# The planner that orders all instructions of a hybrid attention layer gets new durations and a rule on VectorE and GpSimd

## The chip, the cores and the metric

One core of a Trainium2 chip runs the whole layer in one launch. The metric is the device time of one execution in microseconds, lowest is best; the number given for a kernel is the median of its runs. The profile is of one more execution, and it has a time of its own.

## The reference

The layer has 512 tokens of 1024 channels in float32. One RMS-normed input goes through one wide projection; two attention mixers read it, A with 8 heads and B with 8 heads in 2 groups; their outputs are gated, widened to 1024 channels, merged with two sigmoid gates, and projected once more onto the residual.

```python
h = rms_norm(x, norm_w[l])
proj = h @ w_in[l]
(q_a, k_a, v_a, z_a, q_b, kc, vc, ksl, vsl, kwn, vwn, gate_b, z_b, gate_m) = jnp.split(proj, split_points, axis=-1)
o_a = moba_mixer(rms_norm(heads(q_a), q_norm_a[l]), rms_norm(heads(k_a), k_norm_a[l]), heads(v_a), bias_a)
k_cmp = rms_norm(compress(heads(kc), cmp_pos_k[l], cmp_w1_k[l], cmp_w2_k[l]), k_norm_cmp[l])
v_cmp = compress(heads(vc), cmp_pos_v[l], cmp_w1_v[l], cmp_w2_v[l])
o_b = nsa_mixer(...)          # compressed + selected + window branch, each a softmax(q k + bias) v
y_a = o_a * jax.nn.silu(z_a)
y_b = o_b * jax.nn.silu(z_b)
g_m = jax.nn.sigmoid(gate_m)
merged = g_m[..., :D_MODEL] * (y_a @ w_branch_a[l]) + g_m[..., D_MODEL:] * (y_b @ w_branch_b[l])
x = x + merged @ w_out[l]
```

With 512 tokens the block choices of both mixers take in every past block, so A is 8 causal softmax attentions and B is, for each of its 8 heads, two causal softmax attentions (selected and window keys) and a small one over the compressed keys.

## The kernel before

**Arithmetic.** All large products are made as three products of a high and a low part: a weight tile `wr` (128x512) is rounded to `wh`, and `wl = wr - wh` is the rest; the activations are `hh` and `hl`. `mm3` (lines 298 to 312, all its matmuls have line 309) issues hh·wh, hh·wl and hl·wh into one PSUM tile.

**Streams of TensorE work.** Four Python generators issue the matmuls. `gemms` (F) makes the projections in a fixed list: token-major pieces (`pgf`, `pgt`: queries, keys, values), channel-major pieces (`pgc`: gates z and gm), the two widening products (`pbr`, of `yh`/`yl`) and the output (`po`). `attention` (A) walks over 24 units, one softmax attention each: transposed queries and keys (`pq`), scores `sps` for four blocks of query rows from the widest (512 keys) to the narrowest, transposes `pt` of the probabilities `P`, and products with the values into `O`. While unit n makes its scores, unit n-1 makes its transposes and products. `cmp` (C) is the compression of keys and values (`hps`: 16 tiles of `in_w` weights, one after the other, one raw buffer each), and `x_rms` (X) is the token norm.

**The work between matmuls.** Each PSUM tile is followed by a `Chain` of steps on the other engines. A softmax block: `sb` (scores plus bias tile `T`, VectorE, line 848, with the row maximum), exponential `P` (ScalarE, 863, with the row sum), reciprocal (VectorE, 866), scaling of `P` (GpSimd, 867), transposes on TensorE (876), `ph` (ScalarE, 888), `pl` (VectorE, 890), products `O` (910, 1054). A query or key piece: `nraw`, squares, `nss` (554, 353), the power -1/2 `nr` on GpSimd (354), two products `nxn` (556, 551), then high and low part of `qk` (532, 533). After the last product of a head: `ot` (ScalarE, 935), `ys` (939), gate product (949), `yh` (950), `yl` (951); `pbr` of mixer B needs this of all B heads. A weight tile: `wh` (280 or 282) and `wl` (284).

**Who sets the order.** Nothing is reordered by the compiler: `manual_schedule` fixes the order on every engine, and each engine runs its own list strictly in that order. The list is made while the kernel is built, by a small planner in the kernel itself. It keeps a clock `now`, the time at which each engine gets free (`free`), and gives each step a cost in ns; a step that may run on several engines goes to the one that would end first (`Chain.step`); after each step the chain goes on `OUT[engine] + LAT` ns later. The main loop gives the next piece of TensorE work to the stream that is ready and has had least time for its share (`SHARE_A`, `SHARE_F`, `SHARE_C`). The loop before is, in its core:

```python
ok = [r for r, w in ws if w is not None and w <= now[0]]
...
r = min(ok, key=lambda q: q.vt)
```

`W.split(...)`, called by `ahead`, decides how many weight tiles ahead of their use are split. All DMAs are issued by SyncE in the order in which the planner meets them. Four raw weight buffers (`NRAW`), eight split ones, two PSUM tiles for the projections, two for scores, three for transposes and one for `O` bound how far anything can run ahead.

Of the kernel before, what the change touches and what calls it, by code (L numbers as in the profile page):

```python
# [12 lines left out]
F32 = mybir.dt.float32  # L13
# [5 lines left out]
S = 512  # L19
# [22 lines left out]
LAT = 30  # L42
SHARE_A = 1.0
SHARE_F = 1.2
SHARE_C = 0.6
LAG = 20000
XR = 6000.0
XQ = 1200
# [38 lines left out]
def hybrid_kernel(ctx: ExitStack, tc: tile.TileContext, x, xT, norm_w, wtok, wchan, gains, w1,  # L87
# [24 lines left out]
    OUT = {"A": 140, "D": 160, "P": 80}  # L112
# [8 lines left out]
    ENG = {"A": nc.scalar, "D": nc.vector, "P": nc.gpsimd}  # L121
# [7 lines left out]
    def cd(n):  # L129
        return 65 + 1.045 * n  # L130

    def cg(n):
        return 65 + 2.27 * n

    def either(n):
        return {"D": cd(n), "P": cg(n)}

    class Chain:
# [29 lines left out]
        def step(c):  # L168
# [182 lines left out]
    def rsqrt_mean(c, dst, ss, n, w, parts=P):  # L351
        v = (lambda z: z() if callable(z) else z)
        c.do({"D": 70}, lambda e: e.tensor_scalar(v(ss), v(ss), 1.0 / n, EPS, op0=ALU.mult, op1=ALU.add))  # L353
        c.do({"P": 300 + 165 * w}, lambda e: e.tensor_tensor(v(dst), v(ss), mhalf[:parts, :w], op=ALU.pow))  # L354
# [18 lines left out]
    def x_split(k):  # L373
# [4 lines left out]
        c.do({"D": 602}, lambda e: e.scalar_tensor_tensor(hl[:, k, :], xts[k], w, hh[:, k, :].bitcast(F32),  # L378
# [30 lines left out]
    def x_rms():  # L409
# [6 lines left out]
        c = Chain(now[0] + 200)  # L416
        c.do({"D": 70}, lambda e: e.tensor_scalar(rx, ps[:, :NT], 1.0 / D, EPS, op0=ALU.mult, op1=ALU.add), ps)
        c.do({"P": 958}, lambda e: e.tensor_tensor(rx, rx, mhalf[:, :NT], op=ALU.pow))
# [19 lines left out]
    def x_rows():  # L438
# [6 lines left out]
        yield 432  # L445
        Chain(now[0] + 200).do({"A": 478}, lambda e: e.copy(R, ps), ps).mark("R")
# [49 lines left out]
    def gemm_first(name, emit, tags="ggss"):  # L496
# [4 lines left out]
        for k in range(KT):  # L501
            for a, b in ((0, 0), (1, 0), (0, 1)):
# [8 lines left out]
                yield n * 0.4217 * NT + 10  # L511
# [54 lines left out]
    def proj_norm(name, g0, tags="gggg"):  # L566
        toks[name] = [None] * NT

        def emit(t, ps):
            toks[name][t] = att(name)  # L570
            ch = Chain(now[0] + 200)
# [33 lines left out]
    def bias_rows():  # L605
# [28 lines left out]
    def compress_w(kv):  # L634
# [3 lines left out]
        def emit(ps):  # L638
            ch = Chain(now[0] + 200)
# [25 lines left out]
    def compress_h(kv):  # L665
# [4 lines left out]
        for q in range(8):  # L670
            ws = W1.take(1, 256)
            for i in range(2):
# [680 lines left out]
```

## Time and profile before

| | |
|---|---|
| median of 3 runs | 488.29 us (487.93 to 490.03) |
| the profiled execution's own time | 488.61 us |
| its span, first to last instruction | 486.8 us |
| busy share of the span | TensorE 98%, weight loads 88%, VectorE 70%, ScalarE 52%, GpSimd 41% |
| instructions | 8681, of them 3060 matmuls, 831 on VectorE, 625 on ScalarE, 248 on GpSimd |
| granted TensorE clock | 0.999 |

In the profile PE is TensorE's matmuls, PEld its weight loads, DVE is VectorE, ACT is ScalarE, POOL is GpSimd and SP is SyncE. Matmuls overlap in the record, so a busy PE is no proof that it loses nothing; what it loses is read from the waits, or from the distance between starts. "a <- b: 2.9, 5, 1.4" in the view of waits is 2.9 us in five waits of a for b, the longest 1.4 us. A row of the timeline has the start, the duration, the engine, line, operation and tiles, and in brackets the idle time ahead of it with what ended it.

### The profile page before, as it was taken

The page shows a single profiled execution, that of the slowest core. Times are in us where ns is not written, and L with a number is a line of the kernel's source. Part 1 is how long each engine was busy: PE and PEld are TensorE (multiplying, and loading weights), DVE is VectorE, ACT ScalarE, POOL GpSimd, SP SyncE. Part 2 cuts the span into 40 slices and gives each one's busy share as a digit, 9 for nine tenths or more (in the row PEclk, how much of TensorE's full clock was granted, in tenths as well). Part 3 has the DMA queues.
Part 4 walks back from the last instruction along what each step waited for, and adds up shares of the span by engine and source line. Part 5 has one row for each costly group of instructions (what it writes and reads, how often), then busy time and mean ns, then how long its engine had stood idle before and what let it go on. Part 6 is the DMA issues. An engine that isn't in the chain of part 4 may idle for free.

```text
span 486.8 us, 8681 instructions
## 1 busy us (share of the span) xinstructions
PE 474.8 (98%) x3060; PEld 426.5 (88%) x3060; DVE 338.5 (70%) x831; ACT 254.7 (52%) x625; POOL 198.5 (41%) x248
## 2 busy tenths in 40 slices
PE   7999898999999999999999999999999999999997
PEld 7999788999999989988888888888888888889997
DVE  5986898689988769897889777875555535444331
ACT  6565675477785346686675477765222332322210
POOL 4455587257786425856542355554211100110000
PEclk9999999999999999999999999999999999999999
DMA  8548153443343404022212222112223234554421
GB/s 273 160 120 171 42 144 110 131 111 115 110 130 109 131 22 132 22 74 60 65 45 82 92 56 58 42 43 66 65 88 105 91 108 141 148 166 142 140 89 43
DMA packets 28124, 49.16 MB, mean 101 GB/s; under 512 B 3312, under 2 KB 5744, under 8 KB 28080
## 3 DMA queue, kind: packets, MB, share of 16 engines
q1 hardware_dynamic: 28080, 48.60, 35.0%
q8 instruction: 24, 0.39, 0.3%
q14 instruction: 20, 0.16, 0.1%
HBM read 45.84 MB, written 2.75 MB: 100 GB/s over the span
## 4 chain that ended last, share of the span: by engine, by line
PE 73%; DVE 12%; POOL 5%; DMA 4%; issue 3%; ACT 2%; SPq 0%; DVEq 0%; ACTq 0%; POOLq 0%
PE pgc L309 26%; PE po L309 9%; PE pbr L309 9%; PE pgt L309 9%; PE O L910 5%; PE pt L876 5%; PE sps L829 3%; DVE wl L284 2%; PE sps L830 2%; POOL nr L354 2%; DMA rtab<-rt 2%; POOL P L867 1%; PE pq L761 1%; DVE nxn L556 1%; DVE sq L395 1%
## 5 line engine op out<-in xcount | busy, mean ns | idle before, releaser
L309 PE MATMUL pgc<-hh,wh 128*128 128x512 f32 x208 | 84.5, 406 | 0.0
L309 PE MATMUL pgt<-wh,hh 128*128 128x256 f32 (+1 forms) x288 | 82.3, 286 | 0.0
L309 PE MATMUL pgc<-hl,wh 128*128 128x512 f32 x208 | 81.9, 394 | 0.0
L309 PE MATMUL pgc<-hh,wl 128*128 128x512 f32 x208 | 81.8, 393 | 0.0
L284 DVE TENSOR_TENSOR wl<-wr,wh 128x512 fp32r<-128x512 f32 (+1 forms) x101 | 78.9, 784 | 3.6 <-ACT wh L280 3.1
L309 PE MATMUL pgt<-wl,hh 128*128 128x256 f32 (+1 forms) x288 | 81.3, 282 | 0.0
L309 PE MATMUL pgt<-wh,hl 128*128 128x256 f32 (+1 forms) x288 | 81.0, 281 | 0.0
L280 ACT CAST wh<-wr 128x512 fp32r<-128x512 f32 (+1 forms) x91 | 54.1, 616 | 22.9 <-DMA wr<-in_wout 18.1
L284 POOL TENSOR_TENSOR wl<-wr,wh 128x512 fp32r<-128x512 f32 x23 | 31.3, 1361 | 78.9 <-ACT wh L280 78.1
L867 POOL TENSOR_SCALAR P<-P,sst,gate 128x512 f32<-128x512 f32 (+3 forms) x56 | 40.6, 731 | 53.3 <-DVE sst L866 37.2
L848 DVE CUSTOM_DVE_ANT_0 sb<-sps,T 128x512 f32<-128x512 f32 (+3 forms) x96 | 46.3, 485 | 23.0 <-PE sps L830 19.5
L863 ACT ACTIVATE P<-sb,sst 128x512 f32<-128x512 f32 (+3 forms) x88 | 51.0, 580 | 10.8 <-DVE sst L848 7.5
L309 PEld LDWEIGHTS pgt<-wh,hh 128*128 128x128 f32 x288 | 54.2, 188 | 0.5
L309 PEld LDWEIGHTS pgt<-wh,hl 128*128 128x128 f32 x288 | 54.3, 188 | 0.4
L309 PEld LDWEIGHTS pgt<-wl,hh 128*128 128x128 f32 x288 | 54.2, 188 | 0.0
L888 ACT CAST ph<-pt 128x512 fp32r<-128x512 f32 (+2 forms) x72 | 33.6, 479 | 33.5 <-PE pt L876 32.8
L309 PEld LDWEIGHTS pgc<-hl,wh 128*128 128x128 f32 x208 | 39.1, 188 | 9.1
L309 PEld LDWEIGHTS pgc<-hh,wh 128*128 128x128 f32 x208 | 39.1, 188 | 7.2
L309 PEld LDWEIGHTS pgc<-hh,wl 128*128 128x128 f32 x208 | 39.2, 189 | 7.0
L876 PE MATMUL pt<-cst,P 128*128 128x128 f32 x232 | 40.9, 273 | 1.2 <-POOL P L867 1.1
L890 DVE TENSOR_TENSOR pl<-pt,ph 128x512 fp32r<-128x512 f32 (+2 forms) x72 | 38.4, 547 | 4.0 <-ACT ph L888 4.0
L354 POOL TENSOR_TENSOR nr<-nss,mhalf 128x4 f32<-128x4 f32 x28 | 31.0, 1109 | 21.0 <-DVE nss L353 19.3
(214 smaller groups left out, 1108.4 us busy)
## 6 DMA issues: line engine op xcount, KB each, us to landing
wr<-in_wchan SPq DMA_DIRECT2D x52, 256.0 KB, 2.7
wr<-in_wtok SPq DMA_DIRECT2D x36, 256.0 KB, 3.0
T<-rtab SPq DMA_DIRECT2D x16, 256.0 KB, 3.6
wr<-in_w SPq DMA_DIRECT2D x16, 256.0 KB, 2.7
wr<-in_wbr SPq DMA_DIRECT2D x16, 256.0 KB, 2.7
wr<-in_wout SPq DMA_DIRECT2D x16, 256.0 KB, 2.8
x<-in_xT SPq DMA_DIRECT2D x8, 256.0 KB, 4.9
xr<-in_x SPq DMA_DIRECT2D x8, 256.0 KB, 3.6
```

The costliest lines, as they stand in the source:

```text
L280: e.copy(hi, raw)
L284: c.do(either(n), lambda e, hi=hi, lo=lo, raw=raw: e.tensor_sub(lo, raw, hi.bitcast(F32))).mark((w, 1, i))
L309: nc.tensor.matmul(dst, sts[i][a], mvs[i][b], start=(start and i == a == b == 0), stop=(stop and i == n - 1 and b == 1))
L354: c.do({"P": 300 + 165 * w}, lambda e: e.tensor_tensor(v(dst), v(ss), mhalf[:parts, :w], op=ALU.pow))
L829: nc.tensor.matmul(sps[:, :n], qs[:, b * P:(b + 1) * P], ks[:, :n], start=True, stop=False)
L848: e.tensor_tensor_reduce(z["sb"][:, :L], sps[:, :L], T[:, S - L:], scale=-1.0, scalar=3e38, op0=ALU.add, op1=ALU.min, accum_out=st[:, 0, b ...
L863: e.activation(pv(), z["sb"][:, :L], AF.Exp, bias=st[:, 0, b:b + 1], scale=-1.0, accum_out=st[:, 1, b:b + 1])
L867: c.do({"P": 244 + 0.834 * L}, lambda e: e.tensor_scalar(pv(), pv(), st[:, 2, b:b + 1], g, op0=ALU.mult, op1=ALU.mult))
L876: nc.tensor.transpose(pt[:, (b - kb) * P:(b - kb + 1) * P], u.p0 if u.p0 is not None and b == 0 else u.pb[:, POFF[b] + kb * P:POFF[b] + (k ...
L888: e.copy(z["w"][0], pt[:, :w])
L890: ch.do({"D": cd(w)}, lambda e: e.tensor_sub(z["w"][1], pt[:, :w], z["w"][0].bitcast(F32)), pt)
L910: nc.tensor.matmul(O[0][:, S - n:], v.bitcast(F32) if kb == 3 else v, w, start=(u.first and kb == 0 and i == 0), stop=(u.last and kb == 3 ...
```

## The change

No operation is added or removed on TensorE, and no tile, buffer or precision changes. The planner's numbers and two of its rules change, and with them the order of nearly all instructions and the engine of some:

- Costs: GpSimd sums and products go from 65 + 2.27 n to 180 + 2.08 n ns, GpSimd powers from 300 + 165 w to 430 + 150 w, small GpSimd steps from 60 or 82 to 140 or 160, a matmul of n columns from 0.4217 n + 2.5 to 4.5 + 0.4427 n, four transposes from 224 to 340, the delay after TensorE from 200 to 230 ns. After a step a chain waits `OUT + LAT`: 170, 190 and 110 ns for ScalarE, VectorE and GpSimd before, 165, 145 and 90 now.
- Exclusion: steps marked "d" on VectorE and "P" on GpSimd (those that read SBUF operands) exclude each other in the planner's clock; powers and small steps on GpSimd are marked "p" and exclude nothing.
- Shares: F from 1.2 to 1.1 and C from 0.6 to 1.0. A stream counts as ready only when it has been so for 300 ns (`MARGIN`), else the one that has waited longest goes. In the widening products `ahead` counts to 2 instead of 4, so all four next weight tiles are split after the second product instead of two.

```diff
-LAT = 30
+LAT = 60
 SHARE_A = 1.0
-SHARE_F = 1.2
-SHARE_C = 0.6
+SHARE_F = 1.1
+SHARE_C = 1.0
+MARGIN = 300
...
-    OUT = {"A": 140, "D": 160, "P": 80}
+    OUT = {"A": 105, "D": 85, "P": 30}
...
+    lock = {"d": 0.0, "P": 0.0}
...
     def cg(n):
-        return 65 + 2.27 * n
+        return 180 + 2.08 * n
...
     def either(n):
-        return {"D": cd(n), "P": cg(n)}
+        return {"d": cd(n), "P": cg(n)}
+
+    def ends(k, t, n):
+        t = max(t, free[k.upper()])
+        if k in lock:
+            o = lock["d" if k == "P" else "P"]
+            return max(t + n, o + n - 55 if o > t else 0.0)
+        return t + n
...
-                k = min(cost, key=lambda k: max(free[k], c.t) + cost[k])
-                free[k] = max(free[k], c.t) + cost[k]
-                c.t = free[k] + OUT[k] + LAT
+                end, k = min((ends(k, c.t, n), k) for k, n in cost.items())
+                if k in lock:
+                    lock[k] = end
+                free[k.upper()] = end
+                c.t = end + OUT[k.upper()] + LAT
...
-        c.do({"P": 300 + 165 * w}, lambda e: e.tensor_tensor(v(dst), v(ss), mhalf[:parts, :w], op=ALU.pow))
+        c.do({"p": 430 + 150 * w}, lambda e: e.tensor_tensor(v(dst), v(ss), mhalf[:parts, :w], op=ALU.pow))
...
-                ahead((w + 1) / 4)
+                ahead((w + 1) / 2)
...
-        ok = [r for r, w in ws if w is not None and w <= now[0]]
+        ok = ([r for r, w in ws if w is not None and w + MARGIN <= now[0]] or
+              [r for r, w in sorted(((r, w) for r, w in ws if w is not None and w <= now[0]), key=lambda z: z[1])[:1]])
```

Counted over the whole program, TensorE has the same matmuls; VectorE has 31 steps more (17 of them `wl`, 10 `nxn`), GpSimd 37 fewer (17 `wl`, 10 `nxn`, 4 `XW`, 5 copies for `kf`, and others, against 4 more casts), ScalarE 6 more. Line numbers grow by 16 at the places below.

**VectorE, start of the attention.** `sps139` are the first scores, `T` their bias tile (read back from DRAM), `wl138` a weight tile, `nss135` and `nss147`, `nxn134` and `nxn146` the norms of the third and fourth token block of the second query and key piece `qk1`, which the transposes `pq157` need. Before:

```order
L848 ISA sb141_761,sst140_757<-sps139_751,T122_688 128x512
L848 ISA sst140_757 128x1
L284 TENSOR_TENSOR wl138_746<-wr105_611,wh137_745 128x512
L554 TENSOR_REDUCE nss135_738<-nxn134_737 128x4
L866 RECIPROCAL sst140_757<-sst140_757 128x1
L353 TENSOR_SCALAR nss135_738<-nss135_738 128x4
L533 TENSOR_TENSOR qk1109_646<-nxn112_653,qk1109_646 128x4x64
L554 TENSOR_REDUCE nss147_789<-nxn146_788 128x4
L353 TENSOR_SCALAR nss147_789<-nss147_789 128x4
```

Now:

```order
L300 TENSOR_TENSOR wl138_747<-wr105_610,wh137_746 128x512
L570 TENSOR_REDUCE nss135_738<-nxn134_737 128x4
L864 ISA sb141_772,sst140_767<-sps139_761,T123_698 128x512
L864 ISA sst140_767 128x1
L369 TENSOR_SCALAR nss135_738<-nss135_738 128x4
L570 TENSOR_REDUCE nss147_790<-nxn146_789 128x4
L369 TENSOR_SCALAR nss147_790<-nss147_790 128x4
L882 RECIPROCAL sst140_767<-sst140_767 128x1
```

The weight tile, one of the two sums and `qk1109` now stand ahead of the step that waits for `T`; on ScalarE the squares that the second sum reads, and on GpSimd both powers `nr136` and `nr148`, now stand ahead of the first exponential and the first scaling.

**VectorE, the last unit of the attention.** `sb1210` (before) and `sb1218` (now) are its last scores, `pl` the low parts of transposed probabilities, `pbr` a widening product, the two reciprocals those of its blocks of 384 and 256 keys. Before:

```order
L848 ISA sb1210_4908,sst1183_4824<-sps1205_4897,T1135_4659 128x256
L848 ISA sst1183_4824 128x1
L890 TENSOR_TENSOR pl1202_4887<-pt1199_4876,ph1201_4886 128x512
L890 TENSOR_TENSOR pl1207_4901<-pt1203_4890,ph1206_4900 128x384
L866 RECIPROCAL sst1183_4824<-sst1183_4824 128x1
L890 TENSOR_TENSOR pl1212_4915<-pt1208_4903,ph1211_4914 128x256
L866 RECIPROCAL sst1183_4824<-sst1183_4824 128x1
```

Now:

```order
L864 ISA sb1218_4954,sst1193_4873<-sps1210_4938,T1145_4710 128x256
L864 ISA sst1193_4873 128x1
L1222 SCALAR_TENSOR_TENSOR gm953_4017<-gm953_4017,pbr1188_4853 128x512
L906 TENSOR_TENSOR pl1212_4943<-pt1208_4932,ph1211_4942 128x384
L300 TENSOR_TENSOR wl1217_4951<-wr1164_4761,wh1216_4950 128x512
L882 RECIPROCAL sst1193_4873<-sst1193_4873 128x1
L906 TENSOR_TENSOR pl1220_4958<-pt1213_4945,ph1219_4957 128x256
L882 RECIPROCAL sst1193_4873<-sst1193_4873 128x1
```

A gate product and a weight tile now stand between the last scores and the reciprocals.

**TensorE, the end of the attention.** `pt` are the transposes of the last unit's probabilities, `O` its products, `pgc` a gate's projection, `pbr` the widening product. Before, after the last scores, two transposes, six `pgc`, eight steps of the unit before and three `pgc`, the last unit's transposes come, and then

```order
L876 MATMUL pt_4955<-cst,P_4850 128x128 x2
L309 MATMUL pgc_4859<-hh,wh_4798 128x512
L309 MATMUL pgc_4859<-hh,wl_4799 128x512
L309 MATMUL pgc_4859<-hl,wh_4798 128x512
L309 MATMUL pgc_4859<-hh,wh_4798 128x512
L309 MATMUL pgc_4859<-hh,wl_4799 128x512
L309 MATMUL pgc_4859<-hl,wh_4798 128x512
L910 MATMUL O_4924<-ph_4952,vb_2523 128x512
L910 MATMUL O_4924<-pl_4953,vb_2523 128x512
```

and after the last `O` three more `pgc` and the twelve `pbr` of mixer A, ahead of the `pbr` of mixer B. Now, after the last scores, two transposes and eight steps of the unit before:

```order
L892 MATMUL pt_4986<-cst,p_4893 128x128
L892 MATMUL pt_4986<-cst,P_4900 128x128 x3
L892 MATMUL pt_4991<-cst,P_4900 128x128 x3
L892 MATMUL pt_4998<-cst,P_4900 128x128 x2
L926 MATMUL O_4962<-ph_4995,vb_2521 128x512
L926 MATMUL O_4962<-pl_4996,vb_2521 128x512
```

and the twelve `pbr` of mixer B follow the last `O` directly, nine that read earlier heads and three that read the last one's `yh` and `yl`. The projections that stood between are issued earlier, among the units before.

More of the change, by code (lines that the diff above doesn't have):

```diff
@@ L415, in x_rms @@
         yield 856
-        c = Chain(now[0] + 200)
+        c = Chain(now[0] + 230)
         c.do({"D": 70}, lambda e: e.tensor_scalar(rx, ps[:, :NT], 1.0 / D, EPS, op0=ALU.mult, op1=ALU.add), ps)
-        c.do({"P": 958}, lambda e: e.tensor_tensor(rx, rx, mhalf[:, :NT], op=ALU.pow))
+        c.do({"p": 1030}, lambda e: e.tensor_tensor(rx, rx, mhalf[:, :NT], op=ALU.pow))
         c.mark("rx").call(lambda: [fn() for fn in rx_todo])
@@ L570, in emit @@
             toks[name][t] = att(name)
-            ch = Chain(now[0] + 200)
+            ch = Chain(now[0] + 230)
             if name == "kb":
@@ L588, in emit @@
             toks[name][t] = att(name)
-            ch = Chain(now[0] + 200)
+            ch = Chain(now[0] + 230)
             dst, src, r = hl4(toks[name][t]), ps[:, :256].rearrange("p (h d) -> p h d", d=DH), rx[:, t:t + 1]
@@ L618, in f @@
             done["rtab"] = dma(rtab.rearrange("g h v -> h g v"), rt.unsqueeze(1).to_broadcast([16, NG, TW]), 5120)
-            release(rt, now[0] + 2000)
+            release(rt, now[0] + 2300)
         c.call(f)
@@ L638, in emit @@
         def emit(ps):
-            ch = Chain(now[0] + 200)
+            ch = Chain(now[0] + 230)
             for g in range(2):
@@ L678, in compress_h @@
                     W1.split(W1.i + 1)
-                yield 216
+                yield cm(CMPH) * 2
         hs = sp.tile([P, CMPH], F32, name=nm("hs"), tag="c1", bufs=1)
-        c = Chain(now[0] + 200).do({"A": ca(256)}, lambda e: e.copy(hs, hps[:, :256]), hps)
+        c = Chain(now[0] + 230).do({"A": ca(256)}, lambda e: e.copy(hs, hps[:, :256]), hps)
         yield c.ready
@@ L689, in compress_h @@
         t1 = sp.tile([P, P], F32, name=nm("gt"), tag="c2")
-        ch = Chain(now[0] + 200)
+        ch = Chain(now[0] + 230)
         ch.do({"A": 160}, lambda e: e.activation(t1, u, AF.Square))
@@ L715, in compress_k2 @@
         kh = sp.tile([64, 2, DH], F32, name="kh", tag="c6", bufs=1)
-        ch = Chain(now[0] + 200)
+        ch = Chain(now[0] + 230)
         ch.do({"D": 135}, lambda e: e.tensor_scalar_mul(kr, ps[:64, :64], 0.5), ps)
@@ L746, in compress_v2 @@
         vz.extend(vt[:, g] for g in range(2))
-        ch = Chain(now[0] + 200)
+        ch = Chain(now[0] + 230)
         ch.do({"D": 200}, lambda e: e.tensor_scalar_mul(vr, ps[:, :P].rearrange("p (g d) -> p g d", g=2), 0.5), ps)
@@ L780, in k_stack @@
         pt = stack(srcs)
-        yield 224
+        yield 4 * 85
         ks = att("ks")
         kx = att("kx")
-        c = Chain(now[0] + 200)
+        c = Chain(now[0] + 230)
         c.do({"A": 478, "D": 600}, lambda e: copy_on(e, ks, pt.bitcast(F32)))
@@ L830, in qk @@
             nc.tensor.matmul(sps[:, :n], qs[:, b * P:(b + 1) * P], kx[:, :n], start=False, stop=True)
-            yield n * 0.4217 * 2 + 5
-            c = Chain(max(now[0] + 200, tt))
+            yield cm(n) * 2
+            c = Chain(max(now[0] + 230, tt))
             if two:
@@ L881, in tr @@
             yield (4 - kb) * 109
-            ch = Chain(now[0] + 200)
+            ch = Chain(now[0] + 230)
             z = {}
@@ L929, in o_out @@
         y = ys[k]
-        ch = Chain(now[0] + 200)
+        ch = Chain(now[0] + 230)
         z = {}
@@ L999, in pre0 @@
                                      start=True, stop=True)
-                yield 428
-                c = Chain(now[0] + 200)
+                yield 440
+                c = Chain(now[0] + 230)
                 sv = sps[:, :256].rearrange("p (b s c) -> p b s c", b=NT, s=2)
@@ L1126, in f @@
                 e.activation(b["t"], z, AF.Tanh, scale=0.5)
-            ch = Chain(now[0] + 200).do({"D": 602}, lambda e: e.tensor_mul(z, ps, R), ps)
+            ch = Chain(now[0] + 230).do({"D": 602}, lambda e: e.tensor_mul(z, ps, R), ps)
             ch.do({"A": ca(512)}, f, None, "gmt")
-            ch.do({"D": 602}, lambda e: e.scalar_tensor_tensor(z, b["t"], 1.0, z, op0=ALU.add, op1=ALU.mult),
+            ch.do({"d": 602}, lambda e: e.scalar_tensor_tensor(z, b["t"], 1.0, z, op0=ALU.add, op1=ALU.mult),
                   lambda: b["t"])
@@ L1139, in emit @@
         def emit(ps):
[L1140 removed]
+            c = Chain(now[0] + 230).do({"D": 602}, lambda e: e.tensor_mul(t, ps, R), ps)
             gms[w, j] = t, c.do({"A": ca(512)}, lambda e: e.activation(t, t, AF.Tanh, scale=0.5))
```

49 lines of the change are left out of this document (25 added, 24 removed).

## Prediction

> **What bounds the kernel now.** I read the page's busy times first, then the waits of the weight loads, the timeline around each wait, and the chain that ended last.
>
> ```profile
> span 486.8 us, 8681 instructions
> PE 474.8 (98%) x3060; PEld 426.5 (88%) x3060; DVE 338.5 (70%) x831; ACT 254.7 (52%) x625; POOL 198.5 (41%) x248
> ```
>
> TensorE bounds it. Its matmuls stay the same, so the change can only alter the time that TensorE loses. The waits of the weight loads, without those of the first microseconds, hold that loss:
>
> ```profile
> PEld hps L676 <- DVE vl L284: 2.9, 5, 1.4
> PEld pt L876 <- POOL P L867: 2.8, 6, 0.9
> ...
> PEld pq L761 <- DVE qk L533: 1.0, 1, 1.0
> ...
> PEld O L910 <- DVE pl L890: 0.9, 2, 0.7
> PEld po L309 <- DVE wl L284: 0.6, 1, 0.6
> PEld pgf L507 <- DVE hl L378: 0.6, 1, 0.6
> PEld pq L761 <- POOL qk L533: 0.5, 1, 0.5
> ```
>
> Together 9.3 us: that is the most that this change can win if it adds no wait of its own. The chain that ended last gives the pace of undisturbed TensorE work:
>
> ```profile
> 332.29 0.98 PE pt L876 x9
> ...
> 337.01 5.54 PE pbr L309 x24
> ```
>
> A transpose is worth 0.98/9 = 0.109 us, a product of 512 columns 5.54/24 = 0.231 us. With these I turn matmuls that the new order moves into time.
>
> **The change part by part.** *Queries and keys of the second piece (waits 1.0 + 0.5).*
>
> ```profile
> 48.31 0.69 DVE L848 CUSTOM_DVE_ANT_0 sb<-sps,T 128x512 f32<-128x512 f32 x1 [2.68 <-DMA T<-rtab]
> 48.93 0.69 DVE L284 TENSOR_TENSOR wl<-wr,wh 128x512 fp32r<-128x512 f32 x1
> ...
> 51.01 0.42 DVE L554 TENSOR_REDUCE nss<-nxn 128x4 f32<-128x256 f32 x1 [0.40 <-ACT nxn L553]
> 51.07 2.00 POOL L354 TENSOR_TENSOR nr<-nss,mhalf 128x4 f32<-128x4 f32 x2
> ...
> 52.59 0.42 DVE L551 TENSOR_TENSOR nxn<-nxn,gn 128x256 f32<-128x256 f32 x1
> 53.04 0.41 ACT L532 CAST qk<-nxn 128x256 fp32r<-128x256 f32 x1 [2.07 <-DVE nxn L551]
> ...
> 53.64 0.28 PE L761 MATMUL pq<-identr,qk 128*128 128x128 f32 x2
> ...
> 55.49 0.28 PE L761 MATMUL pq<-identr,qk 128*128 128x128 f32 x1 [0.90 <-DVE qk L533]
> ```
>
> VectorE stands 2.68 us before T, with the sums for the norms queued behind. The new order puts one sum, the weight tile and `qk1109` ahead of T. From T on, what is left is 48.31 + 0.69 for `sb`, about 0.2 for the first small step, two powers of 1.0 us, then two products, a cast and a difference of about 0.42 each (1.7), plus 0.1 of handing over: ready at 53.0, needed from 53.64. I take 1.4 of the 1.5. The cover is 0.6 us; if T lands later by more than that, the excess comes back one for one.
>
> *Probabilities (2.8).* Here `pt` waits for GpSimd's scaling of `P`. With 37 fewer steps, casts and differences no longer stand between the scalings, and in the unit that waits at 104 us the TensorE work between last scores and first transposes grows, from 2.6 to 4.1 us by the count of matmuls. In the first unit it stays at 3.9, so part is left: I take 2.0.
>
> *Compression weights (2.9).* Each of the 16 tiles goes through one buffer: a load of 2.7, the cast 0.62 and the difference 0.69, with the issue and handing over some 4.4 us, against 4.4 to 6 us of TensorE work between two uses in the new order. What made them late are differences that took twice their time beside GpSimd:
>
> ```profile
> L280 ACT CAST wh<-wr 128x512 fp32r<-128x512 f32 (+1 forms) x91 | 54.1, 616 | 22.9 <-DMA wr<-in_wout 18.1
> ...
> wr<-in_w SPq DMA_DIRECT2D x16, 256.0 KB, 2.7
> ```
>
> ```profile
> 315.82 1.30 POOL L951 TENSOR_TENSOR yl<-ys,yh 128x512 fp32r<-128x512 f32 x1 [0.50 <-ACT yh L950]
> 316.17 1.50 DVE L284 TENSOR_TENSOR wl<-wr,wh 128x512 fp32r<-128x512 f32 x1
> ...
> 318.06 0.39 PE L910 MATMUL O<-pl,vb 128*128 128x256 f32 x1 [0.42 <-DVE pl L890]
> ```
>
> A `wl` alone takes 0.69, beside `yl` 1.50. With 17 weight differences fewer on GpSimd and the rest kept apart I take 2.2 of 2.9; bounds 0 (the buffer itself is the limit) and 2.9.
>
> [...]
>
> ```profile
> 79.16 0.69 DVE L284 TENSOR_TENSOR wl<-wr,wh 128x512 fp32r<-128x512 f32 x1
> 79.22 1.51 POOL L354 TENSOR_TENSOR nr<-nss,mhalf 128x4 f32<-128x4 f32 x1 [2.04 <-DVE nss L353]
> ```
>
> This power took 1.51 instead of 1.0 beside a `wl`. [...]
>
> *The rest.* The `O` that waited behind the slow `wl`: 0.7 of 0.9. The first projections, where the start's sums and differences move to VectorE and no GpSimd step is left to collide with: 0.6 of 0.6. The output's wait for the third weight tile: split earlier by `ahead`, but the queue behind the gate product stays, so 0.3 of 0.6. Gains: 1.4 + 2.0 + 2.2 + 0.7 + 0.6 + 0.3 = **7.2**.
>
> *New: the end of the attention.* The new order issues F's projections earlier, among the units before. At the last unit it lacks 9 `pgc` between scores and transposes (2.1 us), 6 between transposes and `O` (1.4), 15 products after the last `O` (3.5): 7.0 us of cover are gone. What it covered:
>
> ```profile
> L848 DVE CUSTOM_DVE_ANT_0 sb<-sps,T 128x256 f32<-128x256 f32 x24 | 10.0, 417 | 0.8 <-PE sps L830 0.7
> L863 ACT ACTIVATE P<-sb,sst 128x256 f32<-128x256 f32 x24 | 12.4, 516 | 0.2
> L863 ACT ACTIVATION_READ_ACCUMULATOR P<-sb,sst 128x1 f32 x88 | 17.0, 193 | 0.0
> L866 DVE RECIPROCAL sst<-sst 128x1 f32<-128x1 f32 x96 | 14.5, 155 | 6.0 <-ACT p L863 3.4 <-ACT P L863 2.2
> L867 POOL TENSOR_SCALAR P<-P,sst,gate 128x256 f32<-128x256 f32 x16 | 10.3, 645 | 0.9 <-DVE sst L866 0.9
> L1206 DVE SCALAR_TENSOR_TENSOR gm<-gm,pbr 128x512 f32<-128x512 f32 x16 | 11.0, 688 | 22.6 <-PE pbr L309 22.6
> ```
>
> ```profile
> 332.76 1.24 ACT L888 CAST ph<-pt 128x512 fp32r<-128x512 f32 x3 [1.72 <-PE pt L876]
> 333.38 1.49 DVE L890 TENSOR_TENSOR pl<-pt,ph 128x512 fp32r<-128x512 f32 x3 [2.83 <-ACT ph L888]
> ...
> 335.84 0.48 PE L1054 MATMUL O<-ch,vz 128*128 128x512 f32 x1
> 336.36 0.58 ACT L935 COPY ot<-O 64x512 f32<-64x512 f32 x1 [0.81 <-PE O L1054]
> 336.97 0.69 DVE L939 TENSOR_TENSOR ys<-O,ot 64x512 f32<-64x512 f32 x1 [2.10 <-ACT ot L935]
> ...
> 340.40 0.68 DVE L951 TENSOR_TENSOR yl<-ys,yh 128x512 fp32r<-128x512 f32 x1
> ```
>
> First, the softmax of the last unit: scores plus bias 0.42, exponential 0.52, row sum 0.19, reciprocal 0.16, scaling 0.65 and 0.1 of handing over, so 2.0 us with free engines, against 1.3 us of TensorE work in the new order (eight steps of the unit before and two transposes): 0.7 is lost at least. But the order puts a gate product (0.69), a weight tile (0.69), two `pl` (1.49/3 = 0.50 each) on VectorE ahead of the last reciprocal: 2.0 + 2.4 = 4.4, a loss of 3.1 if all of it lies in the chain. I take 2.5, near that end, because the queue is strict. Second, `ph` and `pl` between transposes and `O`: 1.24/3 + 0.50 = 0.9 and about 0.3 of handing over (an estimate, three steps at 0.1), against the five transposes that follow (0.55): 0.7, and 1.0 if they hide little. Third, the last `O` (done at 336.32) to `yh` and `yl`: `ot` is done 0.62 later, `ys` takes 0.69, the gate product about as much, the cast 0.62 (the row of `wh` above) and handing over 0.4 between them; 3.0 until the first product with `yh` can start. Nine `pbr` of earlier heads (2.1) cover it: 1.0 is left, 1.4 if `yl` (0.68) is late as well. Together **4.2**, bounds 2.4 (0.7 + 0.7 + 1.0) and 5.5 (3.1 + 1.0 + 1.4).
>
> *More work on VectorE.* 31 steps, 17 of them `wl` of 0.69: some 17 us on an engine busy 338.5 of 486.8 us. It is idle 148 us, and slow steps like the 1.50 one get fewer. I add 0.3 for new waits; bounds 0 and the rival below.
>
> Sum: -7.2 + 4.2 + 0.3 = -2.7. The profiled execution took 488.61, its span 486.8 and 1.8 around it; it lies 0.3 above the median of 488.29. So 488.61 - 2.7 = 485.9, on the median's scale **485.6 us**.
>
> **The rivals.** *More is won, less is given back.* All 9.3 us of waits go and the end costs its lower bound 2.4, since loads and VectorE's queue run earlier than the list suggests: 488.29 - 9.3 + 2.4 = 481.4 us. For it: every one of the waits traces to VectorE or GpSimd steps that are slow or queued late. Against: two need a load's landing too.
>
> *The gains are half and the end costs what I say.* The new durations are no truer than the old where it matters (T's landing, the buffer's turn), so the planner's clock drifts as before: 488.29 - 3.6 + 4.2 = 488.9 us, no change that can be measured. This holds, too, if the change does not do what it says. For it: the waits for T and for the weight loads are DMA times, and none of the changed numbers is one.
>
> *Slower: the compression's single buffer becomes the bound.* C's larger share brings its 16 tiles closer, down to 4.4 us of TensorE work, exactly the 4.4 us that a turn takes. If a turn takes 5.3 us on average, because a difference waits behind others on a fuller VectorE (one `wl` ahead is 0.69), about 14 uses wait 0.6 each: 8.4 in place of 2.9, so +5.5, while the other gains are 5.0: 488.29 + 5.5 - 5.0 + 4.2 = 493.0 us. It decides from a turn of about 5 us on. Against: in the trace of before 11 of the 16 tiles are in time, and five are late by 0.58 on average (2.9/5).
>
> **How the numbers follow.** My sum 0.42, more won 0.20, half the gains 0.26, the single buffer 0.12. The likeliest has its own range: gains of 6 to 8.4 and an end of 2.4 to 5.5, each alone within 1.8 of the sum, and both together to 3: 482.6 to 488.6. A measurement of this kernel can tell about 0.5%, 2.4 us, from no change: faster means below 485.85. My sum lies just there, and I give 0.30 of its 0.42 to faster, since the waits are named one by one and the end's largest term is already near its upper bound; with the first rival 0.50. Same: 0.12 and 0.24 of the second rival, 0.36. Slower: 0.02 of that with the end at 5.5, and the third, 0.14. The range goes from the first rival, 481.4, to the second with the end at its upper bound 5.5, 490.2, taken as 490.0; outside lie the third rival and the tail of the first.
>
> **What would show it.** In the waits of the weight loads after: no row of `pq` for `qk` above 0.2, `hps` for `vl` under 1, `pt` for `P` around 0.8 plus a new one in the last unit; no `wl` of 1.5 beside a GpSimd sum. At the end of the attention the timeline should show three idle stretches of TensorE of about 2.5, 0.7 and 1.0, with the reciprocal, `pl` and `yh` or `yl` as releasers. The prediction is wrong if these come to under 2 us, if `hps` waits more than before, or if long waits stand where none of my terms is.

## The result and the profile after

The changed kernel takes 485.76 us in the median of 16 runs (484.32 to 487.85), the kernel before 488.85 us (16 runs, 487.9 to 490.4). The ratio is 0.9932, with a 95% interval of 0.9918 to 0.9947: 0.7% faster, 3.1 us by the medians. The forecast was 485.6 us. The profiled execution of the changed kernel took 486.89 us (span 485.1); it lies 1.1 us above its median, for a reason shown below, so the two profiles differ by only 1.7 us.

The waits of the weight loads in the changed kernel, apart from the first microseconds:

```profile
PEld O L926 <- DVE pl L906: 2.8, 5, 0.9
...
PEld pbr L325 <- ACT yh L966: 1.1, 1, 1.1
...
PEld pt L892 <- POOL P L883: 0.8, 2, 0.5
PEld pgt L325 <- DVE v L608: 0.5, 1, 0.5
PEld po L325 <- DVE wl L300: 0.4, 1, 0.4
PEld pbr L325 <- DVE yl L967: 0.4, 1, 0.4
PEld hps L692 <- DVE vl L300: 0.4, 1, 0.4
PEld pgt L325 <- ACT nraw L560: 0.4, 1, 0.4
...
PEld pq L777 <- DVE pf L784: 0.3, 1, 0.3
```

The rows for `qk` and `hl` are gone, `vl` went from 2.9 to 0.4 and `P` from 2.8 to 0.8. The row for `pl` grew from 0.9 to 2.8, of which 2.6 stand at the end of the attention, and those for `yh` and `yl` are new there. The small rows for `v`, `nraw` and `pf` are new as well.

The start of the attention, from the timeline of three engines, where the kernel before stood 2.68 us for T:

```profile
47.56 0.41 DVE L570 TENSOR_REDUCE nss<-nxn 128x4 f32<-128x256 f32 x1
47.89 0.68 DVE L864 CUSTOM_DVE_ANT_0 sb<-sps,T 128x512 f32<-128x512 f32 x1
```

```profile
48.73 1.99 POOL L370 TENSOR_TENSOR nr<-nss,mhalf 128x4 f32<-128x4 f32 x2 [1.64 <-DVE nss L369]
50.72 0.95 POOL L883 TENSOR_SCALAR P<-P,sst 128x512 f32<-128x512 f32 x1
```

```profile
51.22 0.72 DVE L567 TENSOR_TENSOR nxn<-nxn,gn 128x256 f32<-128x256 f32 x1
51.86 1.16 DVE L549 TENSOR_TENSOR qk<-nxn,qk 128x256 fp32r<-128x256 f32 x2
```

```profile
52.82 0.54 PE L777 MATMUL pq<-identr,qk 128*128 128x128 f32 x4
```

`sb` follows the sum without a gap. That is not the order's doing alone, since the load of T was issued earlier as well. Before and now, from SyncE's rows:

```profile
43.45 0.59 SPq L197 DMA_DIRECT2D T<-rtab  x1
```

```profile
41.81 1.23 SPq L213 DMA_DIRECT2D T<-rtab  x2
```

The two loads of the second row were issued at 41.8 and 42.5 and landed 4.4 to 4.7 us later, so T was there by 47.2 at the latest, before the 47.89 at which `sb` started. How much of the gain is the earlier load and how much the order of VectorE's steps was not separated. The last difference is done at 53.02 and the four transposes from 52.82 on run in a row.

The end of the attention, VectorE and TensorE apart. Units 22 and 23 are the last two:

```profile
328.94 0.41 DVE L864 CUSTOM_DVE_ANT_0 sb<-sps,T 128x256 f32<-128x256 f32 x1
...
329.28 0.68 DVE L1222 SCALAR_TENSOR_TENSOR gm<-gm,pbr 128x512 f32<-128x512 f32 x1
329.88 0.55 DVE L906 TENSOR_TENSOR pl<-pt,ph 128x384 fp32r<-128x384 f32 x1
330.35 0.68 DVE L300 TENSOR_TENSOR wl<-wr,wh 128x512 fp32r<-128x512 f32 x1
330.95 0.15 DVE L882 RECIPROCAL sst<-sst 128x1 f32<-128x1 f32 x1
331.02 0.40 DVE L906 TENSOR_TENSOR pl<-pt,ph 128x256 fp32r<-128x256 f32 x1
```

```profile
329.08 0.50 PE L926 MATMUL O<-pl,vb 128*128 128x512 f32 x1 [0.24 <-DVE pl L906]
...
330.49 0.44 PE L926 MATMUL O<-pl,vb 128*128 128x384 f32 x1 [0.62 <-DVE pl L906]
...
331.48 0.38 PE L926 MATMUL O<-pl,vb 128*128 128x256 f32 x1 [0.43 <-DVE pl L906]
...
332.46 1.97 PE L892 MATMUL pt<-cst,P 128*128 128x128 f32 x8 [0.27 <-POOL P L883]
...
339.73 0.50 PE L325 MATMUL pbr<-yh,wh 128*128 128x512 f32 x1 [0.67 <-ACT yh L966]
```

The gate product and the weight tile stand in VectorE's queue as the order had them. They delay the `pl` of unit 22, so that TensorE waits in that unit's steps, and the reciprocals of unit 23 come while it waits. Eight transposes then take 1.97 us instead of 8 x 0.109 = 0.87. That is the clock, in the rows of the windows (start and end, length, the busy time of PE, PEld, DVE, ACT and POOL with their instructions, the granted clock, the DMA share and GB/s; so the third number from the end is the granted clock):

```profile
328.00:332.40 4.40, 2.90 (x16) 1.76 (x14) 3.49 (x11) 2.66 (x9) 3.49 (x6) 1.00 0.16 53
332.40:335.50 3.10, 3.04 (x12) 2.35 (x12) 1.42 (x3) 1.38 (x3) 1.22 (x3) 0.51 0.27 99
```

After 4.4 us in which TensorE had been busy for 2.9, it ran some 3 us at half its clock. Half of the 16 executions show a mean clock of 0.993 to 0.996, half 0.999 to 1.000; their medians are 486.2 and 485.0 us. The profiled one is of the first half.

### The profile page after: what moved, and what is told of

Its sections match the earlier page's. It is cut to its first block, busy times and chain, and to the rows that moved or that the text cites. A ratio compares the mean times of both kernels' runs of the same rounds, so it can differ in the third digit from the quotient of the medians.

```text
span 485.1 us, 8685 instructions
## 1 busy us (share of the span) xinstructions
PE 475.4 (98%) x3060; PEld 426.7 (88%) x3060; DVE 338.4 (70%) x862; ACT 256.6 (53%) x631; POOL 159.0 (33%) x211
## 4 chain that ended last, share of the span: by engine, by line
PE 95%; DVE 2%; DMA 1%; issue 0%; ACT 0%; POOL 0%; SPq 0%; DVEq 0%
PE pgc L325 30%; PE pgt L325 21%; PE po L325 9%; PE pbr L325 9%; PE O L926 6%; PE pt L892 6%; PE sps L845 3%; PE sps L846 3%; PE pgf L523 3%; PE pq L777 2%; PE hps L692 1%; DMA wr<-in_wtok 1%; PE hps L691 1%; PE scp L1014 1%; PE O L1070 0%
## 5 line engine op out<-in xcount | busy, mean ns | idle before, releaser
L300 DVE TENSOR_TENSOR wl<-wr,wh 128x512 fp32r<-128x512 f32 (+1 forms) x118 | 83.0, 712 | 7.3 <-ACT wh L296 7.0
L298 POOL TENSOR_SCALAR wh<-wr 128x512 fp32r<-128x512 f32 (+1 forms) x34 | 23.3, 687 | 114.9 <-DMA wr<-in_wchan 70.3
L892 PE MATMUL pt<-cst,P 128*128 128x128 f32 x232 | 41.8, 278 | 0.3 <-POOL P L883 0.3
L370 POOL TENSOR_TENSOR nr<-nss,mhalf 128x4 f32<-128x4 f32 x28 | 32.3, 1157 | 21.4 <-DVE nss L369 19.4
```

The costliest lines, as they stand in the source:

```text
L298: e.tensor_scalar(hi, raw, 1.0, 1.0, op0=ALU.mult, op1=ALU.mult)
L300: c.do(either(n), lambda e, hi=hi, lo=lo, raw=raw: e.tensor_sub(lo, raw, hi.bitcast(F32))).mark((w, 1, i))
L370: c.do({"p": 430 + 150 * w}, lambda e: e.tensor_tensor(v(dst), v(ss), mhalf[:parts, :w], op=ALU.pow))
L892: nc.tensor.transpose(pt[:, (b - kb) * P:(b - kb + 1) * P], u.p0 if u.p0 is not None and b == 0 else u.pb[:, POFF[b] + kb * P:POFF[b] + (k ...
```

## The experiments

One more number is used from here on, since it tells places apart: the lost time, worked out from the starts of the matmuls. For each matmul it is the distance to the next start beyond the usual distance (the lower quartile) for the same shapes, of it and its neighbours, in that profile, counted where it is over 0.045 us. Time lost to a lower clock is in it. It comes from one profile each. The last three columns are its sums; the profiled executions' own times differ from the medians.

| kernel | median us | 14 to 322 us | end of the attention | later |
|---|---|---|---|---|
| before | 488.85 | 9.1 | 0 | 1.1 |
| changed | 485.76 | 2.9 | 5.2 | 0.9 |
| e1: six gate projections ahead | 483.26 | 2.8 | 3.7 | 0.9 |
| e2: before, four ahead | 490.83 | 11.5 | 2.3 | 1.1 |
| e3: costs and exclusion alone | 490.26 | 11.4 | 0 | 1.7 |
| e4: shares, margin, split alone | 494.52 | 10.8 | 4.5 | 0.9 |
| e5: seven gate projections ahead | 480.86 | 3.3 | 0 | 0.9 |
| e6: margin 0 | 489.50 | 12.0 | 0 | 0.9 |
| e7: no exclusion | 497.16 | 19.3 | 0 | 1.0 |
| e8: compression's share 0.6 | 485.96 | 3.2 | 4.4 | 0.9 |
| e9: TensorE's idle time filled | 485.35 | 3.1 | 2.9 | 0.9 |
| e10: margin 150 | 483.87 | 7.0 | 0 | 0.9 |
| e11: old GpSimd durations | 488.11 | 7.3 | 2.1 | 0.9 |
| e12: margin 600, eight ahead | 480.30 | 3.3 | 0.1 | 0.9 |

Two profiles of one plan can lose different amounts: before and e2 are the same plan up to 322 us and lost 9.1 and 11.5. Differences under 2.5 us in one column are not read. The changed kernel, e1, e5 and e9 share their plan up to there too and agree within 0.5.

**The end of the attention: e1, e2, e5, e9.**

e1 on the changed kernel:

```diff
-NGM = 5
+NGM = 6
```

> The changed kernel with one number altered: six gate projections instead of five are made ahead of the first widening product (NGM 6). The planned order is the same as the changed kernel's up to TensorE instruction 2013 of 2871; from there nine projections stand again between the last scores and the last unit's transposes, and nine behind them. Theory (the end of the attention gives back what the rest wins, about 4.2 us by my sum, and waits of 4.3 us stand there in the trace after): those waits go and the time falls by 3.5 to 5 us, from 485.8 to about 481.5. Rival (the waits only move: the projections taken for the end are missing somewhere later, or the queue of VectorE is as late there): 484 to 486.

Measured: 483.26 us, ratio to the kernel before 0.9888 (0.9867 to 0.991). In the order that ran, twelve projections stand between the last scores and the transposes, and nine products of mixer A behind those. The waits for `pl` shrank to one of 0.2 us, but the wait for `yh` grew from 1.1 to 2.0:

```profile
PEld pbr L325 <- ACT yh L966: 2.0, 1, 2.0
...
PEld pbr L325 <- DVE yl L967: 0.4, 1, 0.4
```

There `ys` stands behind a gate product and two weight tiles in VectorE's queue, so the second half of the rival, a queue of VectorE that is as late there, had a part of it right: one wait moved. The clock fell again behind this wait:

```profile
339.80:342.80 3.00, 1.44 (x5) 0.60 (x4) 1.92 (x3) 1.14 (x2) 0.34 (x1) 1.00 0.56 175
342.80:346.20 3.40, 3.40 (x10) 2.58 (x9) 2.49 (x4) 0.62 (x1) 0.27 (x1) 0.52 0.22 57
```

Three executions at a mean clock of 1.000 took 482.14 to 482.35 us, three at 0.996 took 484.17 to 484.97, some 2.4 us more; the median lies between the two groups. Even at full clock e1 is 0.8 us above the expected 481.5, about what the wait for `yh` grew by (0.9).

e2 on the kernel before:

```diff
-NGM = 5
+NGM = 4
```

> The kernel before with NGM 4: its planned order is unchanged up to TensorE instruction 2002, and then lacks the projections between the last scores, transposes and products, as the changed kernel does. Theory: the same 3.5 to 5 us are lost, 492 to 494 us, with waits for pl and yh at the end of the attention and none elsewhere. Rival (cover is not what matters there): 488 to 489.5.

Measured: 490.83 us, ratio 1.0043 (1.0027 to 1.0058): 2.0 us more, less than the expected 3.5 to 5. The row for `pl` was 0.9 in two waits, and there was none for `yh`:

```profile
PEld O L910 <- DVE pl L890: 1.9, 4, 0.7
...
PEld pbr L309 <- ACT yh L950: 1.1, 1, 1.1
```

So removing the cover does cost, in the places named, but the price depends on what else stands in VectorE's queue there (in this order the two reciprocals stand ahead of the gate product): 2.3 us of lost time, 4.4 in the changed kernel's (e8, whose end is the same and whose clock was 1.000).

e5 on the changed kernel:

```diff
-NGM = 5
+NGM = 7
```

> As the run with six gate projections ahead, now with seven, so that twelve projections and the products of mixer A stand between the last product of the attention and the products that need its last head. Theory: the 2.4 us that TensorE still waited there for yh and yl go, and with them the stretch of half granted clock (3.3 us at 340 to 346 us) that followed in three of six executions: 479.5 to 480.5 us, and all executions within 1 us of each other. Rival (the dip of the clock has nothing to do with TensorE's idling): the same 2 us less, but half of the executions some 2 us above the rest.

Measured: 480.86 us, ratio 0.9825 (0.9809 to 0.9842), 479.92 to 481.48, every execution at a clock of 1.000. No wait of a weight load is left at the end of the attention. The spread of 1.6 us is larger than expected, with no drop of the clock in it. e5 is 4.9 us faster than the changed kernel: that is what the end of the attention cost there, clock included.

e9 on the changed kernel (`hh` is the normed input's high part; the products are read by nobody):

```diff
+            pvs[0] += 1
...
             for i, w in enumerate(ws):
+                if i == 1 and pvs[0] in IDLE:
+                    if not dm:
+                        dm.append(psum("s", "dm"))
+                    for _ in range(IDLE[pvs[0]]):
+                        nc.tensor.matmul(dm[0], hh[:, 0, :P], hh[:, 0, :], start=True, stop=True)
...
+    pvs, dm, IDLE = [0], [], {90: 3, 91: 3}
```

> The changed kernel, order of all other instructions the same on every engine, with six extra products of 512 columns that nobody reads, three in each of the two longest waits of TensorE for pl at 329 and 331 us (0.78 and 0.60 us long). Theory (TensorE waits there, and it is the idling that makes the granted clock drop to a half for 3.3 us shortly after, which 8 of 16 executions of the changed kernel showed as a mean clock of 0.993 to 0.996): the extra 1.39 us cost nothing, 484.5 to 485.5 us, and executions below 0.998 get rare. Rival (the drop comes from something else): still about half of the executions at 0.996, median 485.5 to 486.5. Rival (the waits are not where the trace has them): 1 us slower.

Measured: 485.35 us, ratio 0.9926 (0.9909 to 0.9944), against 0.9932 for the changed kernel. Six products of 0.231 us went in for nothing, and the wait for `pl` fell by 1.0 (the row was 2.8):

```profile
PEld O L932 <- DVE pl L906: 1.8, 5, 0.6
```

So TensorE really stood idle there. One of six executions had a mean clock under 0.998, where it was 8 of 16; that fits the theory, but six are too few to show it.

**The gains before: e3, e4, e6, e7, e8, e10, e11, e12.**

e3 on the changed kernel (margin, shares and split as before):

```diff
-SHARE_F = 1.1
-SHARE_C = 1.0
+SHARE_F = 1.2
+SHARE_C = 0.6
...
-                ahead((w + 1) / 2)
+                ahead((w + 1) / 4)
...
-        ok = ([r for r, w in ws if w is not None and w + MARGIN <= now[0]] or
-              [r for r, w in sorted(((r, w) for r, w in ws if w is not None and w <= now[0]), key=lambda z: z[1])[:1]])
+        ok = [r for r, w in ws if w is not None and w <= now[0]]
```

> The new durations, delays and the exclusion alone; shares 1.2 and 0.6, the old choice of the ready stream and four steps per weight tile as in the kernel before. Theory (mid-kernel waits go because GpSimd and VectorE collide less and the queues are ordered by truer times): the waits for qk, vl and P fall from 7.2 to under 2.5 us, the end of the attention keeps its projections in the plan, 482 to 484 us. Rival (the ready margin and the shares do it): within 1.5 us of the kernel before.

Measured: 490.26 us, ratio 1.0034 (1.0021 to 1.0047). My theory fails here: with the new durations and the exclusion alone the kernel is slower than before. Its long waits:

```profile
PEld pt L892 <- POOL P L883: 4.5, 7, 1.1
...
PEld hps L692 <- DVE vl L300: 1.8, 3, 0.9
...
PEld pgt L325 <- ACT nraw L560: 1.0, 1, 1.0
PEld pgt L325 <- POOL wl L300: 1.0, 2, 0.6
```

Slow weight differences do not make them, since on VectorE these are as fast as in the changed kernel. Groups by form (the second number behind the bar is the mean in ns) of the kernel before, the changed one and e3:

```profile
L284 DVE TENSOR_TENSOR wl<-wr,wh 128x512 fp32r<-128x512 f32 x97 | 76.0, 786 | 3.5 <-ACT wh L280 3.1 <-POOL wh L282 0.2
...
L284 DVE TENSOR_TENSOR vl<-wr,vh 128x512 fp32r<-128x512 f32 x16 | 12.9, 804 | 0.5 <-ACT vh L280 0.5
```

```profile
L300 DVE TENSOR_TENSOR wl<-wr,wh 128x512 fp32r<-128x512 f32 x114 | 79.7, 708 | 7.3 <-ACT wh L296 7.0
...
L300 DVE TENSOR_TENSOR vl<-wr,vh 128x512 fp32r<-128x512 f32 x16 | 11.9, 746 | 0.7 <-ACT vh L296 0.6
```

```profile
L300 DVE TENSOR_TENSOR wl<-wr,wh 128x512 fp32r<-128x512 f32 x113 | 78.8, 699 | 6.3 <-ACT wh L296 6.0
...
L300 DVE TENSOR_TENSOR vl<-wr,vh 128x512 fp32r<-128x512 f32 x16 | 11.6, 724 | 0.9 <-ACT vh L296 0.7
```

e4, the counterpart, on the kernel before:

```diff
-SHARE_F = 1.2
-SHARE_C = 0.6
+SHARE_F = 1.1
+SHARE_C = 1.0
...
+MARGIN = 300
...
-                ahead((w + 1) / 4)
+                ahead((w + 1) / 2)
...
-        ok = [r for r, w in ws if w is not None and w <= now[0]]
+        ok = ([r for r, w in ws if w is not None and w + MARGIN <= now[0]] or
+              [r for r, w in sorted(((r, w) for r, w in ws if w is not None and w <= now[0]), key=lambda z: z[1])[:1]])
```

> The shares, the margin of 300 ns and the split two tiles ahead alone, with the old durations and no exclusion. Theory: the mid-kernel waits stay at 6 to 9 us and the end of the attention, emptied in this plan too, costs 3.5 to 5: 491 to 494 us. Rival (the rules make the gain): 485 to 487 us.

Measured: 494.52 us, ratio 1.011 (1.0094 to 1.0126). The waits stay (`pt` for `P` is its longest row) and the end of the attention is empty as well:

```profile
PEld pt L877 <- POOL P L868: 4.8, 5, 1.5
PEld hps L677 <- DVE vl L285: 2.6, 3, 1.2
```

Neither half of the change gains anything; together they take 6 us off the loss. That called for a new theory: the margin takes up small lateness, but only where the plan's clock is nearly true. That the new clock is the truer one was not measured step by step.

e6 on the changed kernel:

```diff
-MARGIN = 300
+MARGIN = 0
```

> The changed kernel with a ready margin of 0 instead of 300 ns. The run with the new costs alone lost 11.4 us between 14 and 322 us, the changed kernel 2.9. Theory (a plan with true durations still puts TensorE work at the very instant at which its input is due, and each small lateness becomes a wait; the margin takes it up): the loss before 322 us comes back to 8 to 12 us, and since this plan keeps its projections at the end of the attention the time is 488 to 491. Rival (the shares or the split two tiles ahead are what the costs lacked): loss 3 to 5 us, 481 to 484 us.

Measured: 489.50 us, ratio 1.0007 (0.9993 to 1.0021), lost time before 322 us 12.0. The new theory holds as far as the margin goes, and the shares and the split alone are not what the costs lacked.

```profile
PEld pt L892 <- POOL P L883: 4.6, 8, 1.1
```

e7 on the changed kernel:

```diff
-    lock = {"d": 0.0, "P": 0.0}
+    lock = {}
```

> The changed kernel without the rule that VectorE and GpSimd exclude each other; durations, shares and margin stay. Its plan gives GpSimd 32 steps back and has its end of the attention filled with projections. Theory (the exclusion is what makes the durations true): more steps collide, the loss before 322 us rises from 2.9 to 6 or more, 486 to 490 us. Rival (margin and durations suffice): 481 to 483 us.

Measured: 497.16 us, ratio 1.0162 (1.0146 to 1.0178), lost time 19.3: far beyond what I expected. The new durations without the exclusion are worse than the old ones (e4, 10.8). All four executions have a mean clock of 0.992 to 0.995; in the profile a wait of 2.4 us is followed by a stretch at half clock, which by an estimate from its row (3.40 us at 0.51) holds 1.7 of the 19.3:

```profile
PEld pq L777 <- DVE qk L549: 4.1, 3, 2.4
PEld hps L692 <- DVE vl L300: 4.1, 5, 1.8
```

```profile
58.30:61.70 3.40, 3.40 (x15) 2.98 (x14) 2.55 (x8) 2.70 (x7) 0.00 (x0) 0.51 0.00 0
```

e8 on the changed kernel:

```diff
-SHARE_C = 1.0
+SHARE_C = 0.6
```

> The changed kernel with the compression's share of 0.6 as before; its plan differs from TensorE instruction 829 on. Theory (the waits for vl went because the differences got fast and came in time, not because of the share): hps waits stay under 1 us, and the time is within 1.5 us of the changed kernel, 484.5 to 487.5. Rival (the larger share does it): hps waits of 2 to 4 us, 488 to 490 us.

Measured: 485.96 us, ratio 0.9934 (0.9918 to 0.9949): no difference to the changed kernel, and the waits of `hps` come to 0.8 us. At this resolution the share does nothing for the time.

e10, e11 and e12 on the changed kernel, in this order (e11 has the old numbers of the other powers and small GpSimd steps, too):

```diff
-MARGIN = 300
+MARGIN = 150
```

> The changed kernel with a margin of 150 ns. Its plan has twelve projections behind the last scores, nine behind the last transposes and fifteen behind the last products, as the run with seven gate projections ahead. Theory (the margin takes up lateness in proportion): loss before 322 us between that of 300 ns (2.9) and of 0 (12.0), 5 to 9 us, and 483 to 487 us. Rival (any margin will do, it is the choice of the longest waiting stream that matters): loss 3 us, 480 to 482 us.

```diff
-        return 180 + 2.08 * n
+        return 65 + 2.27 * n
...
-        c.do({"p": 430 + 150 * w}, lambda e: e.tensor_tensor(v(dst), v(ss), mhalf[:parts, :w], op=ALU.pow))
+        c.do({"p": 300 + 165 * w}, lambda e: e.tensor_tensor(v(dst), v(ss), mhalf[:parts, :w], op=ALU.pow))
...
-            c.do({"P": 315 + 0.834 * L}, lambda e: e.tensor_scalar(pv(), pv(), st[:, 2, b:b + 1], g, op0=ALU.mult,
+            c.do({"P": 244 + 0.834 * L}, lambda e: e.tensor_scalar(pv(), pv(), st[:, 2, b:b + 1], g, op0=ALU.mult,
```

> The changed kernel with the old durations of GpSimd's steps (sums 65 + 2.27 n, powers 300 + 165 w, scaling of P 244 + 0.834 n); margin, exclusion and all other durations new. Its end of the attention is filled as in the run with six gate projections ahead. Theory (durations matter beside exclusion and margin; scalings of P planned 71 ns too short and powers 70 too short): loss before 322 us of 5 to 9 us, 485 to 489 us. Rival (70 ns are inside the margin of 300): loss 2.5 to 4 us, 482 to 484 us.

```diff
-NGM = 5
+NGM = 8
...
-MARGIN = 300
+MARGIN = 600
```

> The changed kernel with a margin of 600 ns and eight gate projections ahead, so that the end of the attention is filled. Theory (300 ns already cover most of the lateness; more leaves less work to choose from): loss before 322 us of 2 to 4 us, 480 to 482 us. Rival (still more is won): under 2 us of loss, 478 to 480 us. Rival (too large a margin starves TensorE): 484 us or more.

Measured: e10 483.87 us (ratio 0.9893, 0.9877 to 0.991) with 7.0 us lost; e11 488.11 (0.9987, 0.9971 to 1.0004) with 7.3, at the upper part of what was expected; e12 480.30 (0.9822, 0.9801 to 0.9843) with 3.3. A margin of 0, 150, 300 and 600 ns loses 12.0, 7.0, 2.9 and 3.3 us before 322 us. With the old GpSimd durations the longest wait there is again that of the powers' chain, and a margin of 300 doesn't reach it; a stretch from 56.0 to 59.6 us at a clock of 0.53 follows it, which by the same estimate holds 1.7 of the 7.3. In the medians e11 is 4.9 us slower than e1, whose end of the attention shows the same waits for `yh` and `yl`:

```profile
PEld pq L777 <- DVE qk L549: 2.0, 1, 2.0
```

e12 and e5 beat both kernels, by 1.8% against the kernel before; their intervals overlap, and which of them is the better one stays open.

## Why the prediction was right, and where its reasons were not

The time, the sign and the size came out: 485.6 forecast, 485.76 measured. An agreement to 0.2 us is luck beside the parts: by the lost times 6.2 were won between 14 and 322 us and 5.2 given back at the end, so these two stretches give 1.0 of the 3.1 us between the medians, and one plan profiled twice differed by 2.4. Step by step:

- *Queries and keys: 1.4 forecast.* All 1.5 gone, in the trace as the order has it; this step was not undone alone. The chain was forecast to end at 53.0 and ended at 53.02, which is luck in the last digits: `sb` started 0.42 earlier than I took, with T loaded earlier, and the steps behind the powers took 2.30 (from 50.72 on) in place of 1.8. A product took 0.72 beside the scaling of `P` (the one ahead of it, at 50.76, took 0.43), and of the two differences at 51.86 the one beside a cast on GpSimd took 0.83, the other 0.41. The two powers themselves took 1.99, as I took it. So two steps of VectorE beside one of GpSimd were slow in this chain, 0.72 and 0.83, and both are steps that I had counted at 0.42 each; the product at 50.76, beside the same scaling, was not slow, and what tells the two products apart was not shown. The cover of 0.6 did not exist, either: TensorE had lost less by then and came at 52.82 instead of 53.64. Over the whole program the powers got a little slower: 1157 ns in the mean instead of 1109. No TensorE wait for `qk` stands in the waits.
- *Probabilities: 2.0.* 2.8 fell to 0.8, of which 0.5 is the new wait in the last unit, so 2.5 of the old ones are gone. The reason failed here, too: e3 has exactly as few steps on GpSimd (211) and waits 4.5 for `P`.
- *Compression weights: 2.2.* 2.5 gone, but **this step failed in its reason**. I wrote that what made them late were differences that took twice their time beside GpSimd. The trace before already speaks against it: the five late differences took 0.69, 1.11, 0.68, 0.63 and 1.51 us, for waits of 0.2, 1.4, 0.3, 0.6 and 0.3. Only two were slow, and what they took beyond 0.69 explains at most 0.7 of the 2.9. Slow ones did get rare (15 of 97 `wl` of 512 columns took over 0.9 us before, 5 of 114 now), but in e3 they are as rare (4 of 113), and it still waited 1.8 us for `vl`, as e6 did. What e3 and e6 lack and the changed kernel has is the slack that the margin puts into the plan.
- *The rest: 0.7, 0.6, 0.3.* The `O` behind the slow `wl` and the first projections are rid of their waits; the output's wait fell by 0.2.
- *New waits: 0.3.* The rows for `v`, `nraw` and `pf` come to 1.2 us: mis-sized by 0.9.
- *The end of the attention: 4.2.* Lost time 4.4 us at full clock (e8). Of the three places the first shows its loss in the `pl` of unit 22 and not at the transposes of unit 23, since `pl` stands behind the same gate product and weight tile; its size is near the 2.5 (0.40, 0.78 and 0.60 us by the starts, and 0.5 for `P`). The second, `ph` and `pl` behind the transposes, cost 0.8 by the starts in e8 where 0.7 was forecast. For `yh` 1.0 was forecast; the rows have 1.1 for the weight load, and 0.4 for `yl`.
- *Not in the sum:* the half clock, some 1.2 us between the two halves of the executions.

The larger error is one that the sum hides. I explained the gains by less contention and a better queue from truer numbers, and the margin of 300 ns stands in none of my gains. e3 and e4 show that each half of the change alone gains nothing, e6 that the margin carries the gain, e7 that it does so only with the exclusion in the planner's clock, and e11 that most of it goes without the new GpSimd durations. And e6 against the changed kernel shows that the margin also empties the end of the attention: with 0 the plan kept its projections there. What I read from the new order came out because it held the joint effect; the causes that I named for the waits before 322 us were not the ones that the runs show. The reading of the end of the attention held in its cause as well: e1 and e5 fill it and win, and e9 finds TensorE idle where the trace has the waits.

Each setting is one plan. How much a plan's loss moves by chance, with a number changed that means nothing, was not measured; the steps of the series from 0 to 300 ns (5.0 and 4.1 us) and the halves are larger than the scatter seen here (2.4 us between two profiles of one plan, 0.3 between the plans of e8 and the changed kernel), but 3.3 against 2.9, or e11's 7.3 against e10's 7.0, says nothing.

## What to carry to other kernels

Here a static order needed two things at once: a clock that includes the collisions (before 322 us 2.9 us lost with the exclusion, 19.3 without it in e7), and slack for what the clock gets wrong (12.0 lost with a margin of 0 in e6). Test such things together, since either alone can look useless or harmful. When a planner spends independent work earlier, look where the order runs out of it: here two gate projections more ahead of the first widening product, so that work is left for the end of the attention, were worth 4.9 us, more than the whole change. A reason that fits every wait is still to be tested by undoing it.

## What the runs showed of the hardware

In these runs TensorE lost its clock without standing still for long. In the changed kernel no single wait ahead of the drop was over 0.9 us, and 2.9 us of work in 4.4 us were followed by some 3.1 us at a clock of 0.51; in e1 a wait of 2.0 us was followed by 3.4 us at 0.52, beginning about 1 us after work had resumed, and e7 and e11 show such a stretch behind waits of 2.4 and 2.0 us for `qk`. Only part of the executions of the changed kernel and e1 have a mean clock under 0.998 (8 of 16, 3 of 6), and in e8, with the waits of the changed kernel, and in e11 behind the wait of 2.0 us for `yh`, the profile has no drop. What sets the drop is not shown by these runs. TensorE did not have to be idle for as long as the clock then stayed low: in the changed kernel, of all stretches of 3.4 us (the slow one of e1 was 3.40 long) ahead of the drop, the one in which TensorE worked least still had it busy for 2.06 us.

```profile
328.84:332.25 3.41, 2.06 (x9) 1.23 (x9) 2.65 (x9) 1.92 (x7) 2.50 (x4) 1.00 0.16 52
```

In executions of the kernel before, a mean clock of 0.995 to 0.997 occurred too (7 of the 17 beside e1, 488.43 to 490.25 us, against 488.13 to 490.11 for the rest) without costing time that can be seen, and in one of five of e10, whose end of the attention is filled; where it falls there was not found.

The first microseconds differ from execution to execution as well. Work done by 13.6 us in the changed kernel and in e5, whose orders are the same there (the first pair of numbers is TensorE's busy time and its matmuls):

```profile
0.00:13.60 13.60, 10.41 (x69) 10.15 (x70) 7.79 (x13) 10.12 (x18) 1.74 (x9) 1.00 0.88 273
```

```profile
0.00:13.60 13.60, 10.92 (x83) 10.66 (x84) 8.15 (x13) 10.35 (x17) 1.02 (x9) 1.00 0.86 274
```

Fourteen matmuls lie between them, and 1.6 us of lost time (2.9 and 1.3 up to there, reckoned as above, short losses included), which is as much as the spread of e5's times; what sets it was not tried.
